# A two-block model in one kernel: parameters of a norm and splits ahead of a loop, a pair's one-hot product earlier, later posts, and products of ones in five waits

## The chip, the cores and the metric

The kernel runs on one core of one Trainium2 chip. The metric is the time of one execution on the device in microseconds, the median of several runs. Instructions run on TensorE (PE; the loads of its weights are told apart as PEld), VectorE (DVE), ScalarE (ACT) and GpSimd (POOL); SyncE (SP) issues most of the DMA transfers.

## What is computed

256 tokens of width 1024, float32, pass through two blocks of two layers each. A layer of the first block is a mixer (pooling, short convolution, attention) and a gated feed-forward, both behind an RMS norm that is modulated by a vector `c`. A layer of the second block is a mixer with three kinds of attention and then a mixture of 16 experts of width 512, each followed by a layer norm:

```python
def hybrid_layer(x, c_act, ...):                     # the first block runs it twice
    sh1, sc1, g1, sh2, sc2, g2 = jnp.split(c_act @ w_ada + b_ada, 6)
    h = rmsnorm(x, norm1_w) * (1 + sc1) + sh1
    u = h @ w_in
    ...
    x = x + g1 * (merged @ w_out)
    h2 = rmsnorm(x, norm2_w) * (1 + sc2) + sh2
    return x + g2 * ((silu(h2 @ w_gate) * (h2 @ w_up)) @ w_down)

def second_block(x, ...):
    h = layer_norm(x, ln_in_g, ln_in_b)
    for l in range(2):
        mix = mixer_sublayer(h, ...)
        h = layer_norm(ALPHA * h + mix, ln1_g[l], ln1_b[l])
        h = layer_norm(ALPHA * h + grouped_moe(h, ...), ln2_g[l], ln2_b[l])
    return h

def grouped_moe(h, ...):
    scores = sigmoid(h @ router_w)       # a group of 4 experts is chosen, then 2 of the 4
    ...
    for e in range(16):
        a = silu(h @ w_gate[e]) * (h @ w_up[e])
        y = y + dense_gates[:, e:e + 1] * (a @ w_down[e])
    return y
```

## The kernel before

The state (`st[0]`, 256 tokens as two tiles of 128 partitions) stays in SBUF. The order of PE's instructions is the order in which the program is written; a scheduler sets the order of DVE, ACT, POOL and SP. Each engine works its own instructions strictly in order. To put work of one stage into the waits of another, the program keeps a list `steps` of generators and a list `posts`; `pump` (L110) first runs all posts, then some steps.

**First block.** Products in float32 are made of two halves of higher and lower bits: weights are split by a CAST on ACT and a subtraction on DVE (L278, L279, tile `split`) and multiplied at L289, L290 and L321 to L323. `ada_pe` makes the modulation; its transposes at L685 wait for a product by DVE at L682. In the first layer (L908 on) the products of `w_in` begin behind the first modulation.

**Mixer of the second block** (`mixer`, L1193). It begins with the layer norm: `norm_params` (L806) makes scale and shift of each token out of the aggregates of statistics that were taken on the fly, `normalise` (L819) applies them on ACT and DVE, PE transposes the result (L855), and `ev` (L1202) writes it in two halves to `hl`. Then come the low-rank products of `w_in`, by L321 to L323.

**Mixture of experts** (`moe`, L1475). The routing is small work on DVE (L1506 to L1530) that ends in the masks `mb` and `mask`. Five products on PE (L1534 to L1538) count the places of the tokens in each expert, `one_hot` (L1546) makes matrices of 128 tokens by 64 places for each of four experts, and `gather` (L1562) picks the tokens with them, out of the normalised state in two halves `hn`; the lower halves are subtractions on POOL (L1502) and DVE (L1569).

The 16 experts go in 8 pairs (`pair`, L1619): the two experts' 64 places each fill the 128 partitions. `proj` (L1592) makes the gate and the up product out of 8 k-chunks of weights, the activation (L1632 to L1634) is transposed by PE (L1638) and copied by ACT (L1640), and two projections of 512 columns follow (four of 256 for the last pair), which ACT and DVE evict as two halves `yh` and `yl`, scaled by `gs` (L1671, L1672). `combine_T` (L1602) multiplies the one-hot by the gates (`go`, L1607), transposes it on PE (L1612) and derives `got` and `gs` from it. `combine` adds the pair's result to the state: a product of `got` and `yh`, `yl` (L1655) and an add on DVE (L1657). Its two steps are run by `pump` in the next pair, between L1634 and the transposes and after L1640; in the last pair, each quarter's is called from `proj` of the next quarter, behind its first k-chunk, with the statistics for the next norm (L802) behind it. The weights, 6.3 MB a pair, come in pieces of 1 MB on SP's queue (L1683) into a ring of 18 units.

If an expert has more than 64 tokens, the pairs are run again in a loop of rounds (`tc.For_i`, L1716), whose count is read from memory (L1710); in the runs here its body isn't entered, but every engine passes through its branch. `norm_params` for the next norm stands behind this loop, and at the very end the last norm with its gains (L1743 to L1761).

## Time and profile before

| | |
|---|---|
| time, median of 3 runs | 1619.72 us (1618.51 to 1620.62) |
| time of the profiled execution | 1618.68 us |
| span of its trace, first to last instruction | 1616.4 us |
| PE busy | 1510.0 us (93%), 9211 instructions |
| DVE busy | 976.5 us (60%) |
| ACT busy | 736.3 us (46%) |
| POOL busy | 251.8 us (16%) |
| DMA | 419.71 MB, 260 GB/s on average |
| mean granted clock of PE | 0.980 |

Shares are of the span. The second block begins near 841 us; its two expert stages lie from about 985 to 1219 and from about 1370 to 1602. A row of a timeline has the start of a group of like instructions, the time from the first's start to the last's end, engine, line, operation, and in brackets the idle time of the engine before it and what ended that. The granted clock is PE's: 1.00 is 2.4 GHz, 0.50 is 1.2 GHz.

### The profile page before, as it was taken

Reading aid. Unit: us, or ns where it says so; the run is one execution under the profiler, and the core shown is the slowest. Engines: PE = TensorE matmul, PEld = TensorE weight load, DVE = VectorE, ACT = ScalarE, POOL = GpSimd, SP = SyncE. Lnnn points to the kernel's source line nnn. Section 1 sums busy time; section 2 is a strip of 40 time slices with the busy share of each in tenths; the row PEclk is TensorE's granted clock in tenths of the full one; section 3 lists DMA queues with packets and bytes.
Section 4 is the critical chain, followed back from the end, with each engine's and each line's share of the span. In section 5 each row is a group of like instructions: output and inputs, shape, how many; then the busy total and the mean of one; then the engine's idle time right before and its main releaser. Section 6 shows DMA issues by size and latency. Waiting matters only on the chain. (4 is left out here: it accounts for less than half of the span.)

```text
span 1616.4 us, 24413 instructions
## 1 busy us (share of the span) xinstructions
PE 1510.0 (93%) x9211; PEld 1092.7 (68%) x9211; DVE 976.5 (60%) x1894; ACT 736.3 (46%) x1403; POOL 251.8 (16%) x279
## 2 busy tenths in 40 slices
PE   6999999999999999999989998999988998999996
PEld 5877888888887888888878775334437776344332
DVE  4869777777786767777557774322137767222224
ACT  3466645655456664556446664112115565111112
POOL 0334640001242363000003100000001210000000
PEclk9999999999999999999999998999998999999998
DMA  9766769557854675965526368999985558899992
GB/s 346 245 215 236 261 219 353 181 179 235 313 186 136 218 271 185 318 207 174 164 73 209 128 222 300 403 407 407 407 314 168 179 180 315 314 407 406 407 405 92
DMA packets 278476, 419.71 MB, mean 260 GB/s; under 512 B 12722, under 2 KB 147748, under 8 KB 278348
## 3 DMA queue, kind: packets, MB, share of 16 engines
q1 hardware_dynamic: 273052, 398.63, 69.5%
q0 software_dynamic: 5152, 19.14, 3.4%
q8 instruction: 77, 1.26, 0.3%
q14 instruction: 51, 0.42, 0.1%
q10 hardware_dynamic: 144, 0.26, 0.0%
HBM read 416.94 MB, written 1.05 MB: 259 GB/s over the span
## 5 line engine op out<-in xcount | busy, mean ns | idle before, releaser
L279 DVE TENSOR_TENSOR split<-raw,split 128x1024 fp32r<-128x1024 f32 (+4 forms) x330 | 411.7, 1251 | 114.3 <-ACT split L278 111.2
L289 PE MATMUL mm<-hl,split 128*128 128x512 f32 x1168 | 412.6, 397 | 0.0
L278 ACT CAST split<-raw 128x1024 fp32r<-128x1024 f32 (+4 forms) x330 | 328.7, 1000 | 131.6 <-PE mm L323 69.5
L290 PE MATMUL mm<-hl,split 128*128 128x256 f32 x1168 | 326.3, 279 | 1.0 <-DVE split L279 1.0
L289 PEld LDWEIGHTS mm<-hl,split 128*128 128x128 f32 x1168 | 219.0, 187 | 50.4 <-issue 0.7
L1597 PE MATMUL mm<-raw,xg 128*64 128x512 f32 x1024 | 230.9, 602 | 1.1 <-ACT xg L1564 1.1
L290 PEld LDWEIGHTS mm<-hl,split 128*128 128x128 f32 x1168 | 220.3, 189 | 1.5 <-DVE split L279 1.3
L1597 PEld LDWEIGHTS mm<-raw,xg 128*64 128x64 f32 x1024 | 71.5, 138 | 136.5 <-issue 118.7
L289 PE MATMUL mm<-ahl,split 128*128 128x512 f32 x352 | 123.4, 395 | 0.0
L306 ACT COPY t<-mm 128x256 f32<-128x256 f32 x152 | 56.4, 371 | 142.7 <-PE mm L290 133.7
L1597 PE MATMUL mm<-raw,t 128*64 128x512 f32 (+1 forms) x576 | 114.8, 549 | 1.4 <-ACT t L1640 1.4
L321 PE MATMUL mm<-split,hl 128*128 128x512 f32 (+4 forms) x272 | 102.3, 376 | 4.2 <-ACT split L278 3.2
L290 PE MATMUL mm<-ahl,split 128*128 128x256 f32 x352 | 98.3, 279 | 0.3 <-DVE split L279 0.3
L322 PE MATMUL mm<-split,hl 128*128 128x512 f32 (+4 forms) x272 | 96.4, 355 | 1.0 <-DVE split L279 1.0
L323 PE MATMUL mm<-split,hl 128*128 128x512 f32 (+4 forms) x272 | 96.4, 355 | 0.3 <-POOL hl L1210 0.2
L306 DVE TENSOR_TENSOR t<-mm,t 128x256 f32<-128x256 f32 x140 | 59.1, 422 | 47.9 <-ACT t L306 47.7
L1633 DVE SCALAR_TENSOR_TENSOR t<-t,mm 128x512 f32<-128x512 f32 x16 | 11.0, 686 | 123.3 <-ACT t L1632 123.3
L1597 PEld LDWEIGHTS mm<-raw,t 128*64 128x64 f32 x576 | 39.4, 137 | 63.8 <-issue 53.4
L1672 DVE SCALAR_TENSOR_TENSOR t<-mm,s,t 128x512 fp32r<-128x512 f32 (+1 forms) x36 | 24.9, 692 | 94.9 <-ACT t L1671 94.9
L1671 ACT ACTIVATE t<-mm,s 128x512 fp32r<-128x512 f32 (+1 forms) x36 | 23.0, 640 | 129.9 <-PE mm L1597 129.9
L289 PEld LDWEIGHTS mm<-ahl,split 128*128 128x128 f32 x352 | 66.0, 187 | 15.5 <-ACT t L1095 0.2
L1640 ACT COPY t<-at 128x512 f32<-128x512 f32 x16 | 9.4, 586 | 129.7 <-PE at L1638 129.7
(426 smaller groups left out, 2563.3 us busy)
## 6 DMA issues: line engine op xcount, KB each, us to landing
raw<-in_exp_w_gate_dram SPq DMA_DIRECT2D x128, 512.0 KB
raw<-in_exp_w_up_dram SPq DMA_DIRECT2D x128, 512.0 KB
raw<-in_exp_w_down_dram SPq DMA_DIRECT2D x128, 512.0 KB
raw<-in_w_in_dram SPq DMA_DIRECT2D x54, 1024.0 KB
raw<-in_w_ada_dram SPq DMA_DIRECT2D x30, 1024.0 KB
raw<-in_w_gate_dram SPq DMA_DIRECT2D x22, 1024.0 KB
raw<-in_w_up_dram SPq DMA_DIRECT2D x22, 1024.0 KB
ada<-in_w_ada_dram POOLq DMA_DIRECT2D x18, 1024.0 KB, 5.8
```

What stands on the lines that cost most here:

```text
L278: S.copy(h, src)
L279: V.tensor_sub(lo, src, h)
L289: PE.matmul(ps, h[:, k], x[k0 + k], start=first and k == 0, stop=False)
L290: PE.matmul(ps[:, :T], lo[:, k], x[k0 + k][:, :T], start=False, stop=last and k == K - 1)
L306: return S.copy(b[:, :T], ps[:, T:]), V.tensor_add(dst, ps[:, :T], b[:, :T])
L321: PE.matmul(ps[i][:, :n], xh, h[:, j], start=f, stop=False)
L322: PE.matmul(ps[i][:, :n], xh, lo[:, j], start=False, stop=False)
L323: PE.matmul(ps[i][:, :n], xl, h[:, j], start=False, stop=z)
L1597: PE.matmul(ps[64 * b:64 * b + 64, :], lhs(k, b), ws[k][b], start=k == 0, stop=k == nk - 1)
L1633: V.scalar_tensor_tensor(th, th, 1.0, pg, op0=OP.add, op1=OP.mult)
L1671: S.activation(yh[:, sl], pd_[:, :w], AF.Copy, scale=gs)
L1672: V.scalar_tensor_tensor(yl[:, sl], pd_[:, :w], gs, yh[:, sl], op0=OP.mult, op1=OP.subtract)
```

## The change

It has six parts. (1) `pump` runs a post only if it was there at the pump before. (2) `busy(n)` puts n products of a matrix of ones, 128x128 by 128x512 in bfloat16, on PE, into a bank that nobody reads: 12 in the first layer behind the first modulation, 12 behind the first `normalise`, 10 and 2 around the routing's products, 8 ahead of the loop of rounds, 4 behind the other `normalise`. (3) In `mixer`, the transposes of quarters 2 and 3 become steps that run between the chunks of the first low-rank product. (4) POOL's subtractions of the routing become two on DVE, one ahead of the mask's products, one behind `one_hot`. (5) `combine_T` is a generator: `go` is made at the pair's beginning, the transposes come at the fourth k-chunk of the gate product, in the last pair too; the combine of a quarter also moves to the fourth k-chunk, and the last pair pumps as the others do. (6) `norm_params` and the first splits of the next `w_in` stand ahead of the loop of rounds (and `norm_params` again in its body); in the last layer the gain banks are copied to SBUF there, and the last norm reads these copies instead of PSUM.

```diff
     def pump(n=1):
-        while posts:
+        for _ in range(min(aged[0], len(posts))):
             posts.pop(0)()
+        aged[0] = len(posts)
...
+    def busy(n, w=512):
+        pb = at_bank()
+        for _ in range(n):
+            PE.matmul(pb[:, :w], onesb, onesb[:, None, :].to_broadcast([P, w // P, P]), start=True, stop=True)
...
             ada_pe(0, 2, ada_first[2])
-            pump()
+            while posts:
+                posts.pop(0)()
+            busy(12)
...
-        transposed(ev)
+        transposed(ev, (0, 1))
+        def rest():
+            for q in (2, 3):
+                transposed(ev, (q,))
+                yield
+        steps.append(rest())
...
-        rq = rank_in(xs_gemm(k_chunks(W, l, KD, 0, 384), hl, 384), 384, cqT, 3, "mla_q")
+        rq = rank_in(xs_gemm(k_chunks(W, l, KD, 0, 384), hl, 384, 1), 384, cqT, 3, "mla_q")
...
-                    if q == 0:
-                        G.tensor_sub(hn[1][:, i, sl], y[:, i, sl], hn[0][:, i, sl])
...
+        V.tensor_sub(hn[1][:, 0, 0:512], y[:, 0, 0:512], hn[0][:, 0, 0:512])
         gained = gains(f"ln1_{l}", [mm_bank(), mm_bank()])
         next(gained)
+        busy(10)
         pp = at_bank()
...
+        busy(2)
...
         oh = one_hot(0, pos)
+        V.tensor_sub(hn[1][:, 1, 0:512], y[:, 1, 0:512], hn[0][:, 1, 0:512])
...
-                if mid and k == 1:
+                if mid and k == 3:
                     mid()
...
+            yield
             pb = at_bank()
             for i in range(2):
                 PE.transpose(pb[:, i * P:(i + 1) * P], go[:, i * P:(i + 1) * P], ident)
...
-            return got, gs[:, 0:1]
+            yield got, gs[:, 0:1]
...
-            if done:
-                got, gs = combine_T(p, oh)
+            turned = combine_T(p, oh)
+            next(turned)
+            box = []
             pg, pu = mm_bank(), mm_bank()
-            proj(pg, xs, wg, KD, more=more)
-            if done:
-                pump(2)
+            proj(pg, xs, wg, KD, lambda: box.extend(next(turned)), more)
+            got, gs = box
...
-            if not done:
-                got, gs = combine_T(p, oh)
...
+        keep = sml.tile([P, 8], F32, tag="keep", name=nm("keep"), bufs=1)
+        norm_params(keep)
+        busy(8)
+        splits[:] = U_SPLIT
+        nsplit[0] = 0
         if l + 1 < L:
-            mixer_first(l + 1)
+            wf = mixer_first(l + 1)
+            split_early(wf[0][1][:, 0:2])
+            split_early(wf[0][1][:, 2:4])
+            taken = ring["units"] + U_SPLIT[:2]
+        else:
+            lnb = unit(U_LAST, "lnb").rearrange("p (v q n) -> p v q n", v=2, q=2)
+            for q in range(2):
+                for v in range(2):
+                    pb = gain_bank(f"ln2_{l}", v, q)
+                    (S.copy if v else V.tensor_copy)(lnb[:, v, q], pb)
+            taken = (U_LAST,)
...
     normalise(*norm_params(), st.pop())
+    busy(12)
     for l in range(L):
-        moe(l, mixer(l))
+        keep = moe(l, mixer(l))
         if l + 1 < L:
-            held[:] = 3 * [normalise(*norm_params())]
-    g_, b_ = [[gain_bank(f"ln2_{L - 1}", v, q) for q in range(2)] for v in range(2)]
-    rs, nb = norm_params()
...
+            normalise(keep[:, 4:6], keep[:, 6:8])
+            busy(4)
...
-            V.scalar_tensor_tensor(t, t, mean[:, i:i + 1], g_[q], op0=OP.add, op1=OP.mult)
-            V.scalar_tensor_tensor(t, t, rs[:, i:i + 1], b_[q], op0=OP.mult, op1=OP.add)
+            V.scalar_tensor_tensor(t, t, mean[:, i:i + 1], lnb[:, 0, q], op0=OP.subtract, op1=OP.mult)
+            V.scalar_tensor_tensor(t, t, rs[:, i:i + 1], lnb[:, 1, q], op0=OP.mult, op1=OP.add)
```

The changed file has other line numbers: L1597 of before is L1616 there, L1607 is L1626, L1615 and L1616 are L1635 and L1636, L1634 is L1654, L1655 and L1657 are L1673 and L1675, L1672 is L1690, L279 is L288, L802 is L811, the aggregates of L810 are L817.

DVE within one pair of experts, before (`t_10456` is the pair's activation, `t_10483` its `go`, the adds at L1657 belong to the pair before):

```order
L1634 SCALAR_TENSOR_TENSOR t_10456<-t_10455,mm_10422 128x512
L1657 TENSOR_TENSOR state_8374<-state_8374,at_10460 128x512
L1657 TENSOR_TENSOR state_8374<-state_8374,at_10464 128x512
L1657 TENSOR_TENSOR state_8374<-state_8374,at_10475 128x512
L1657 TENSOR_TENSOR state_8374<-state_8374,at_10479 128x512
L1607 TENSOR_TENSOR t_10483<-oh_10186,gate_10204 128x128 x2
```

DVE from the activation of one pair to that of the next, after the change (`t_10623` is the next pair's `go`):

```order
L1654 SCALAR_TENSOR_TENSOR t_10506<-t_10505,mm_10465 128x512
L1675 TENSOR_TENSOR state_8387<-state_8387,at_10510 128x512
L1675 TENSOR_TENSOR state_8387<-state_8387,at_10514 128x512
L1675 TENSOR_TENSOR state_8387<-state_8387,at_10525 128x512
L1675 TENSOR_TENSOR state_8387<-state_8387,at_10529 128x512
L1690 SCALAR_TENSOR_TENSOR t_10543<-mm_10533,s_10476,t_10542 128x512
L1690 SCALAR_TENSOR_TENSOR t_10556<-mm_10546,s_10476,t_10555 128x512
L1626 TENSOR_TENSOR t_10623<-oh_10559,gate_10244 128x128 x2
L1635 TENSOR_SCALAR got_10649<-at_10646 128x256
L1636 TENSOR_REDUCE s_10650<-at_10646 128x1
```

The instruction that makes `go` has moved from behind the four adds to behind the evictions of the pair before.

PE in the last pair's projections by quarters, before (`mm_11455` is the first quarter, `mm_11468` the second, `t_11464` and `t_11465` are `yh` and `yl` of the first):

```order
L1597 MATMUL mm_11455<-raw_11369,t_11451 64x256 x8
L1597 MATMUL mm_11468<-raw_11372,t_11451 64x256 x2
L1655 MATMUL at_11471<-t_11464,got_11387 128x256
L1655 MATMUL at_11471<-t_11465,got_11387 128x256
L1655 MATMUL at_11477<-t_11464,got_11387 128x256
L1655 MATMUL at_11477<-t_11465,got_11387 128x256
L1597 MATMUL mm_11468<-raw_11372,t_11451 64x256 x6
```

And after the change:

```order
L1616 MATMUL mm_11495<-raw_11409,t_11483 64x256 x8
L1616 MATMUL mm_11508<-raw_11412,t_11483 64x256 x6
L1673 MATMUL at_11515<-t_11504,got_11435 128x256
L1673 MATMUL at_11515<-t_11505,got_11435 128x256
L1673 MATMUL at_11521<-t_11504,got_11435 128x256
L1673 MATMUL at_11521<-t_11505,got_11435 128x256
L1616 MATMUL mm_11508<-raw_11412,t_11483 64x256 x2
```

Six instead of two products of the next quarter now stand ahead of the combine (each of these rows' products at L1597 appears as two instructions in the trace).

DVE at the end of the first expert stage, before (L1710 is the read of the count of rounds, L1716 the loop's branch):

```order
L1657 TENSOR_TENSOR state_8374<-state_8374,at_11539 128x256
L802 BN_STATS s_11475<-state_8374 128x6 x2
L1710 TENSOR_LOAD nri_10215
L1716 COMPARE_AND_BRANCH
```

And after the change:

```order
L811 BN_STATS s_11519<-state_8387 128x6 x2
L817 BN_AGGR keep_11598<-s_11519 128x2
L288 TENSOR_TENSOR split_11623<-raw_11619,split_11623 128x768
L817 BN_AGGR keep_11598<-s_11519 128x2
L288 TENSOR_TENSOR split_11626<-raw_11619,split_11626 128x768
L821 TENSOR_SCALAR s_11602<-keep_11598 128x2
L823 SCALAR_TENSOR_TENSOR s_11603<-s_11601,s_11602 128x1 x2
L824 SCALAR_TENSOR_TENSOR keep_11598<-s_11603,s_11601 128x2
L825 SCALAR_TENSOR_TENSOR keep_11598<-keep_11598 128x2
L1728 TENSOR_LOAD nri_10255
L1750 COMPARE_AND_BRANCH
```

The norm's chain and two splits have moved ahead of the loop's branch, between the two aggregates and behind them.

## Rows read from the trace of the kernel before

**Rows 1.** The page, busy time of each engine over the span.

```profile
PE 1510.0 (93%) x9211; PEld 1092.7 (68%) x9211; DVE 976.5 (60%) x1894; ACT 736.3 (46%) x1403; POOL 251.8 (16%) x279
```

**Rows 2.** The waits of PE: line, releaser, us in total, times, longest.

```profile
PE at L1612 <- DVE t L1607: 18.0, 14, 1.8
...
PE at L1534 <- DVE mb L1530: 9.0, 2, 4.5
PE at L685 <- DVE t L682: 6.4, 3, 3.4
```

**Rows 3.** Timeline, a middle pair of experts, and the beginning of pair 7.

```profile
1065.64 2.65 DVE L1657 TENSOR_TENSOR state<-state,at 128x512 f32<-128x512 f32 x4
...
1068.64 0.44 PE L1612 MATMUL at<-con,t 128*128 128x128 f32 x2 [1.20 <-DVE t L1607]
...
1187.15 0.53 PE L1612 MATMUL at<-con,t 128*128 128x128 f32 x2 [1.77 <-DVE t L1607]
```

**Rows 4.** Timeline, the last pair of the first expert stage, PE.

```profile
1194.62 2.13 PE L1655 MATMUL at<-t,got 128*128 128x512 f32 x8
...
1196.69 7.09 PE L1597 MATMUL mm<-raw,xg 128*64 128x512 f32 x32
...
1204.57 0.66 PE L1638 MATMUL at<-con,t 128*128 128x128 f32 x4 [0.79 <-DVE t L1634]
...
1205.90 2.38 PE L1597 MATMUL mm<-raw,t 128*64 128x256 f32 x20 [0.68 <-ACT t L1640]
...
1214.73 1.14 PE L1655 MATMUL at<-t,got 128*128 128x256 f32 x4
...
1217.89 1.14 PE L1655 MATMUL at<-t,got 128*128 128x256 f32 x4 [0.57 <-ACT t L1671]
```

**Rows 5.** By windows: length, busy times, PE's clock, DMA share, GB/s.

```profile
1160.00:1180.00 20.00, 18.80 (x93) 8.11 (x93) 5.07 (x10) 3.27 (x6) 0.00 (x0) 1.00 1.05 407
1180.00:1200.00 20.00, 18.23 (x84) 6.70 (x82) 5.74 (x11) 1.97 (x3) 0.00 (x0) 1.00 1.07 394
1200.00:1220.00 20.00, 16.01 (x102) 8.07 (x98) 8.03 (x21) 4.06 (x7) 0.00 (x0) 1.00 0.20 73
```

**Rows 6.** Timeline, the routing of the first expert layer.

```profile
985.71 2.50 POOL L1502 TENSOR_TENSOR hn<-state,hn 128x512 fp32r<-128x512 f32 x2 [46.25 <-ACT hn L1500]
...
986.07 0.93 DVE L1524 TENSOR_TENSOR s<-s,s 128x8 f32<-128x8 f32 x1
987.03 1.22 DVE L1530 SCALAR_TENSOR_TENSOR mb<-s,s 128x32 bf16<-128x32 f32 x1
...
988.17 0.18 DVE L1530 SCALAR_TENSOR_TENSOR mask<-s,s 128x32 f32<-128x32 f32 x1
...
991.54 3.68 PE L1597 MATMUL mm<-raw,xg 128*64 128x512 f32 x8
```

**Rows 7.** The first layer's first product (timeline), and windows behind it.

```profile
27.22 0.79 PE L321 MATMUL mm<-split,hl 128*128 128x512 f32 x1 [3.25 <-ACT split L278]
...
30.00:32.00 2.00, 2.00 (x6) 1.57 (x5) 1.09 (x1) 0.00 (x0) 0.00 (x0) 0.50 1.05 410
32.00:34.00 2.00, 2.00 (x8) 1.60 (x7) 0.00 (x0) 0.70 (x1) 0.00 (x0) 0.81 1.05 409
```

**Rows 8.** Timeline, PE at the beginning of the second block's first mixer.

```profile
842.51 3.67 PE L855 MATMUL at<-con,state 128*128 128x128 f32 x16 [3.15 <-ACT state L826]
```

**Rows 9.** Timeline, behind the loop of rounds of the first expert layer.

```profile
1222.47 0.39 DVE L810 BATCH_NORM_AGGREGATE s<-s 128x2 f32<-128x24 f32 x2 [2.22 <-issue]
...
1224.86 3.68 PE L855 MATMUL at<-con,state 128*128 128x128 f32 x16 [5.83 <-ACT state L826]
...
1228.19 0.96 DVE L279 TENSOR_TENSOR split<-raw,split 128x768 fp32r<-128x768 f32 x1 [0.57 <-ACT split L278]
```

**Rows 10.** Timeline, the last norm.

```profile
1608.40 1.41 DVE L1758 SCALAR_TENSOR_TENSOR state<-state,s,at 128x512 f32<-128x512 f32 x2 [2.15 <-ACT t L1748]
...
1610.01 1.27 POOL L1750 TENSOR_TENSOR state<-state,t 128x512 f32<-128x512 f32 x1 [239.32 <-ACT state L1749]
```

More of the change, by code (lines that the diff above doesn't have):

```diff
@@ L108 @@
     steps, posts = [], []
+    aged = [0]
     def pump(n=1):
-        while posts:
+        for _ in range(min(aged[0], len(posts))):
             posts.pop(0)()
+        aged[0] = len(posts)
         while n and steps:
@@ L174 @@
     RING_MOE = (22, 8, 10, 11, 0, 12, 13, 9, 17, 18, 19, 20, 21, 5, 6, 7, 3, 4)
+    U_LAST = 12
     UNIT = {8: 2560}
@@ L802, in stats, with norm_params @@
             V.bn_stats(bs[0][:, i, 6 * q:6 * q + 6], src[i] if src else st[0][:, i, w * q:w * q + w])
-    last_mv = [None]
-    def norm_params():
-        mv = last_mv[0] = small(4).rearrange("p (a b) -> p a b", a=2)
+    def norm_params(keep=None):
+        mv = (keep[:, 0:4] if keep is not None else small(4)).rearrange("p (a b) -> p a b", a=2)
         for i in range(2):
             V.bn_aggr(mv[:, i], bs[0][:, i])
-        y, h, z, rs, nb = small(2), small(2), small(2), small(2), small(2)
+        y, h, z = small(2), small(2), small(2)
+        rs, nb = (small(2), small(2)) if keep is None else (keep[:, 4:6], keep[:, 6:8])
         S.activation(y, mv[:, :, 1], AF.Abs_reciprocal_sqrt, bias=epst[:, 2:3])
@@ L1710, in moe @@
         rounds = nc.values_load(nri[0:1, 0:1], min_val=1, max_val=4)
-        if l + 1 < L:
-            mixer_first(l + 1)
-        loop_ring = tuple(u for u in RING_MOE if l + 1 == L or u not in ring["units"])
+        keep = sml.tile([P, 8], F32, tag="keep", name=nm("keep"), bufs=1)
[3 more added lines that the diff above has]
+        nsplit[0] = 0
+        if l + 1 < L:
+            wf = mixer_first(l + 1)
[9 more added lines that the diff above has]
+            taken = (U_LAST,)
+        loop_ring = tuple(u for u in RING_MOE if u not in taken)
         first_ring = ring["units"]
@@ L1727, in moe @@
                 stats(q, new=False, n=4)
+            norm_params(keep)
         if l + 1 < L:
@@ L1730, in moe @@
             mixer_ahead(l + 1)
+            return keep
+        return keep, lnb
     first = mixer_first(0)
@@ L1735 @@
     normalise(*norm_params(), st.pop())
+    busy(12)
     for l in range(L):
-        moe(l, mixer(l))
+        keep = moe(l, mixer(l))
         if l + 1 < L:
-            held[:] = 3 * [normalise(*norm_params())]
-    g_, b_ = [[gain_bank(f"ln2_{L - 1}", v, q) for q in range(2)] for v in range(2)]
-    rs, nb = norm_params()
-    mean = small(2)
-    V.tensor_scalar_mul(mean, last_mv[0][:, :, 0], -1.0)
+            normalise(keep[:, 4:6], keep[:, 6:8])
+            busy(4)
+    keep, lnb = keep
+    mean, rs, nb = keep[:, 0:4:2], keep[:, 4:6], keep[:, 6:8]
     t = st[0][:, 1, 0:512]
-    gb = [t512() for _ in range(2)]
-    for s_, d_ in zip((g_, b_), gb):
-        S.copy(d_, s_[0])
     S.activation(t, t, AF.Identity, bias=nb[:, 1:2], scale=rs[:, 1:2])
-    G.tensor_mul(t, t, gb[0])
-    G.tensor_add(t, t, gb[1])
+    G.tensor_mul(t, t, lnb[:, 0, 0])
+    G.tensor_add(t, t, lnb[:, 1, 0])
     for q in range(2):
```

## The prediction

> **What bounds the kernel now.** I read the page's first lines, then the list of what TensorE (PE) waited for, then the timeline and the tables by stretch at each place the diff touches. PE is busy 1510.0 us of a 1616.4 us span [rows 1], so I look for the places where PE stands still or runs slowly, and ask what each edit does there. The list of waits shows three of them [rows 2]: the combine's transposes at L1612 (14 waits, 18.0 us in all), the routing's products at L1534 (two waits, 9.0) and the modulation at L685 (three, 6.4). Four more come from timelines: the first layer's first product, the beginning of each mixer, the loop's gate, and the end.
>
> The sum is made against the profiled execution, 1618.68 us; the median of the runs, 1619.72, is 1.04 above it.
>
> **Combine, 14 pairs.** Before, PE needs the transposes of `go` right after the activation's transposes and two combine steps of the pair before. VectorE (DVE) makes `go` behind four adds that hold it 2.65 us from 1065.64, and PE waits 1.20 for it; ahead of pair 7 it waits 1.77 [rows 3]. Six pairs at 1.2 and one at 1.77 make 9.0 a layer, the 18.0 of the list. After the change `go` stands on DVE right behind the previous pair's last `yl`, and PE asks for it at the fourth k of the gate projection. Eight k's take 7.09 us [rows 4], so three take 2.66. Pair 7 shows how soon `go` can be had: 1.77 us behind the product before it. So it is there before PE asks: **-18.0** (-12, if 0.4 stayed at each of the 14, to -18.0). Next late are the weights, below.
>
> **The last pair.** PE waits 0.79 at its activation transposes and 0.68 at its first down product. After the change two combine steps of pair 6 (8 products, 2.13 us, which before ran ahead of the up product) stand around these two places and fill them: 1.47 a layer, **-2.9** (0 to -2.9). The quarters of the last down product follow each other at 3.16 us (1214.73 to 1217.89). Of it 16 instructions of projection take 1.90 (20 took 2.38), and four combine products 1.14, waiting included, since they stand two products behind the quarter that they read, too early for `yl`. With six products between, that wait is covered. A combine product alone takes between 0.13 (half of one with 512 columns, 2.13 / 8) and 0.285 (1.14 / 4); at 0.2, between the two, a round is 2.7: 0.45 less, three times, and a little at the last: -1.5 a layer, **-3.0** (-0.4 to -4.4) [rows 4].
>
> **Weights.** In the experts' stage the queues move 407 GB/s, 394 between 1180 and 1200, and after 1200 only 73 x 20 us = 1.46 MB, about what the next layer's first two loads hold. So the last expert bytes land near 1200 [rows 5]. A piece of 1.05 MB takes 2.57 us at 407. Counted back over the four pieces of the last down weights, the last up piece lands near 1190; PE uses it at about 1202, at 6 of 8 k's behind 1196.69 [rows 4]. Of this slack of 11.6 us the change takes 9.0 (the waits) and 2.13 (the combine steps, now behind the up product). Half a microsecond is left; for pieces that come a little late I charge **+0.6** (0 to +11, rival B).
>
> **Routing, twice.** POOL's two subtractions hold 985.71 to 988.21. Beside them a DVE instruction of 128x8 took 0.93, and the one that makes `mb` 1.22, while its twin, the next on DVE, made `mask` in 0.18 [rows 6]. The subtractions move to DVE, one ahead of `mb` at 0.66, as one of the four adds took [rows 3]. So DVE saves 0.75 and 1.04, pays 0.66, and with some overlap lost `mb` comes 0.4 earlier, at least in the likeliest case. Then the clock: the first 8 products of the gate projection took 3.68 us [rows 6], where 8 of 32 take 1.77 [rows 4]; 12 products of ones now run in the wait of 4.5. No row shows such a product; nearest is the combine's of 128x512, 0.27, so 12 take 3.2 and fit. If they hold the clock, 1.9 comes back here and about 0.5 in the gather ahead of it: -2.8 with the 0.4. Half of the clock's part counted, -1.8 each: **-3.6** (+0.4 to -5.6).
>
> The Trainium skill, "SBUF — State Buffer", section "Who interferes with whom", has it that a VectorE instruction with two SBUF inputs and a GpSimd instruction that reads SBUF shut each other out for a whole instruction. The 0.93 and 1.22 beside 0.18 agree.
>
> **First layer and first mixer.** The first product of the first layer comes at 27.22 behind a wait of 3.25; the granted clock is 0.50 after it and 0.81 on average from 32 to 34, so it is back at about 32.8 [rows 7]. From 28 to 32.8 half speed costs 2.4. Twelve products of ones run in the wait; but the weights land at 410 GB/s all the while and can hold PE next: **-1.5** (0 to -2.5). At mixer 0, behind a wait of 3.15, 16 transposes take 3.67 [rows 8], 0.23 each, against 0.165 for the four of the last pair [rows 4]. At that pace they cost 1.0 less, at double speed 1.8; half of them also move behind the first products: **-2.0** (-0.5 to -2.7). The 12 products, 3.2, just fit the wait.
>
> **The loop's gate.** At the branch DVE stands 2.22 us, then the aggregates come at 1222.47, and PE's transposes, behind a wait of 5.83, at 1224.86; the first split on DVE at 1228.19 [rows 9]. After, the chain from the aggregates to the normalising (about 1.5 of these 2.39) and two split subtractions (2 x 0.96) stand ahead of the branch on DVE; behind it there are two split subtractions less and half the transposes ahead of the first product. So the normalising begins some 1.7 later than it would with the branch alone, less the chain and the table load that no longer follow: what is paid and what is gained nearly cancel. **-0.5** for mixer 1 (+1.5 to -2.0).
>
> **End.** The first two of six last DVE instructions take 1.41 from 1608.40, with one operand in PSUM; POOL multiplies from 1610.01 for 1.27, and adds after it [rows 10]. After, the parameters are there before the branch, and the gain banks are copied to SBUF there: some 0.85 earlier. But now both operands lie in SBUF, as in the slow pair [rows 6], and DVE can stand for up to 2 x 1.27 = 2.5. I take **+1.0** (-0.9 to +1.7). By the same section of the Trainium skill's "SBUF — State Buffer" the whole 2.5 would be paid and the sum be 0.7 higher; no run here shows it for these shapes.
>
> **Posts.** The modulation's posts come one pump later; three waits of 6.4 in all [rows 2] leave PE, but DVE and POOL set that loop's period: **-0.5** (+0.5 to -3.0).
>
> Sum: -18.0 - 2.9 - 3.0 + 0.6 - 3.6 - 1.5 - 2.0 - 0.5 + 1.0 - 0.5 = -30.4. 1618.68 - 30.4 + 1.04 = **1589.3 us**.
>
> **Rivals.**
> B, the weights bind. From about 1000 to 1190 the queue works 190 us without a break. At the 394 of its last stretch instead of 407 [rows 5] the last up piece lands 6 us later; less the 0.5 of slack, 5.5 a layer, 11 in all: 1600. For it: the slack is nearly used up. Against: 407 is steady before.
> C, the products of ones don't hold the clock. Then the 1.5 of the first layer, the 2.0 of mixer 0 and 2.8 of the routing's 3.6 fall away: 1595.6. For it: no row shows the clock under such products.
> D, slower. PE frees the ring's units at other moments than the loads want them, and the expert queue falls behind. Its point: per layer the loads come 17 us later over the 190, a rate near 374; each of the two stages then ends 5.4 later than before and, less the 7.6 that lie outside the weights' reach (1.5, 2.0, 3.6, 0.5), the kernel is 3.2 slower: 1623. At 366 it is 1631. Against: no wait that goes away holds a load back, and no window of the stage shows such a rate.
> E, all small places give their upper ends: 1.4 (quarters) + 2.0 (routing) + 1.0 + 0.7 + 1.5 + 1.9 + 2.5 = 11.0 more: 1578.
> N, it doesn't do what it says: DVE reaches `go` behind the adds again, and the 18.0 stay: 1607.3. Against: in the order `go` stands ahead of them.
>
> **Numbers.** Forecast 0.60, B 0.15, C 0.13, E 0.05, N 0.02, D 0.05 (0.03 of it beyond 0.2%). A measurement of this kernel can tell 0.2%, 3.2 us, from no change. Faster: 0.60 + 0.15 + 0.13 + 0.05 + 0.02 = 0.95; within it 0.02; slower 0.03. The range takes in C and most of B above, and reaches to E below: 1579 to 1603. Outside lie D, N, about half of E and a third of B, 0.15 in all.
>
> **What would show it.** Right: no wait at the `go` transposes, and none for a weight transfer in its place; rounds of 2.7 us in the last pair; the first gate step at 1.8 to 2 us, `mb` near 0.2, mixer 0's transposes at half their time, full granted clock near 30 us. B and D would show as waits of PE for expert weights, C as granted clock 0.5 at the same places, E as waits gone at L685. Last DVE instructions longer than 0.75 beside POOL would show the contention at the end. Waits that move from `go` to the combine's adds or the activation, so that the two stages don't shrink by some 12 us each, would make the prediction wrong.

## The result, and the profile after

The changed kernel takes 1598.73 us, the median of four runs from 1593.02 to 1602.77, beside 1619.12 for the kernel before on the same chip: a ratio of 0.9875, 95% interval 0.984 to 0.9911. It is faster, by 20 us where 30 were forecast; the time lies inside the range of 1579 to 1603 and 9.4 above the forecast. The profiled execution took 1599.32 us, its span is 1597.3. Line numbers of the changed kernel are higher than before's by 9 in the first block and by some 18 in the expert stage.

What PE waits for now (line, releaser, us in total, times, longest):

```profile
PE mm L1077 <- DVE t L1082: 6.0, 6, 1.0
...
PE at L135 <- issue: 5.5, 1, 5.5
PE mm L1079 <- DVE split L288: 4.3, 5, 1.4
...
PE mm L332 <- POOL hl L1220: 2.7, 5, 0.9
...
PE at L1551 <- DVE mb L1545: 1.5, 1, 1.5
```

The waits for `go` and, but for 0.2 us, for the modulation's product [rows 2] are gone, and of the routing's 9.0 us 1.5 are left (L1551). In their place stand six at the merged products (L1077; before, two of 1.8 in all) and 4.3 us for splits beside them (L1079), five at a mixer's first products (L332), and 5.5 us ahead of products of ones (L135) behind the loop of rounds.

The timeline of a middle pair, of the beginning of pair 7 and of the last pair:

```profile
1050.72 0.44 PE L1632 MATMUL at<-con,t 128*128 128x128 f32 x2
...
1179.48 0.48 DVE L1626 TENSOR_TENSOR t<-oh,gate 128x128 f32<-128x128 f32 x2
1180.55 0.44 PE L1632 MATMUL at<-con,t 128*128 128x128 f32 x2
...
1193.31 0.60 PE L1658 MATMUL at<-con,t 128*128 128x128 f32 x4
1193.66 1.18 PE L1673 MATMUL at<-t,got 128*128 128x512 f32 x4
1194.77 3.24 PE L1616 MATMUL mm<-raw,t 128*64 128x256 f32 x28
1197.94 0.74 PE L1673 MATMUL at<-t,got 128*128 128x256 f32 x4
...
1200.49 0.74 PE L1673 MATMUL at<-t,got 128*128 128x256 f32 x4
```

No bracket stands behind the transposes at L1632 now, where before's had 1.20 and 1.77 [rows 3]. The quarters of the last pair follow each other at 2.55 us (1197.94 to 1200.49) instead of 3.16 [rows 4], and four combine products take 0.74, as they no longer wait inside.

The routing of the first expert layer:

```profile
984.92 2.33 PE L135 MATMUL at<-onesb 128*128 128x512 bf16 x10
...
988.46 0.18 DVE L1545 SCALAR_TENSOR_TENSOR mb<-s,s 128x32 bf16<-128x32 f32 x1
...
991.92 2.59 PE L1616 MATMUL mm<-raw,xg 128*64 128x512 f32 x8
```

The products of ones fill 2.33 us of PE's wait, `mb` takes 0.18 instead of 1.22, and the first eight gate products take 2.59 instead of 3.68 [rows 6].

PE at the loop of rounds behind the first expert stage:

```profile
1204.94 1.14 PE L1673 MATMUL at<-t,got 128*128 128x256 f32 x4 [0.58 <-ACT t L1689]
1205.97 1.89 PE L135 MATMUL at<-onesb 128*128 128x512 bf16 x8
1213.36 1.89 PE L135 MATMUL at<-onesb 128*128 128x512 bf16 x4 [5.51 <-issue]
1215.05 0.85 PE L863 MATMUL at<-con,state 128*128 128x128 f32 x3
```

The next mixer's transposes begin 10.11 us behind the last combine (1204.94 to 1215.05), where before it was 6.97 (1217.89 [rows 4] to 1224.86 [rows 9]).

The windows of the end of the first expert stage (length, busy times, PE's clock, DMA share, GB/s):

```profile
1160.00:1180.00 20.00, 20.00 (x94) 7.49 (x92) 5.81 (x10) 2.56 (x4) 0.00 (x0) 1.00 1.05 407
1180.00:1200.00 20.00, 20.00 (x116) 9.20 (x114) 6.67 (x14) 3.71 (x6) 0.00 (x0) 1.00 1.07 394
```

PE is busy without a gap, where it was 18.80 and 18.23 of 20 [rows 5], and the transfers keep the same two rates. No wait of PE for expert weights is in its list.

To see where the time went I took, from the traces, the starts of the same PE instructions in two kernels, and from their differences how much each stretch got longer (+) or shorter (-) against the kernel before, in us. The stretches: **merged**, the merged products of the second layer (586 to 617); **mixer**, from the last transposes of the first block to the end of the second block's first low-rank product; **routing** 0 and 1, from the router's last product to the fourth step of the gate product; **experts** 0 and 1, from there to the last combine; **loop**, from there to the end of the next first low-rank product; **end**, from the last combine to the end of the span. "E" rows are the experiments below.

| | merged | mixer | routing 0 | experts 0 | loop | routing 1 | experts 1 | end |
|---|---|---|---|---|---|---|---|---|
| changed kernel | +3.4 | -0.3 | -1.4 | -12.7 | +6.4 | -2.5 | -11.9 | +0.3 |
| E1 no ones | +2.6 | +2.0 | -1.4 | -12.7 | +3.5 | -0.7 | -12.2 | -0.4 |
| E2 loop as before | +2.6 | -0.2 | -2.6 | -11.7 | +3.2 | -2.5 | -11.1 | +0.3 |
| E3 posts as before | -0.2 | -0.2 | -2.5 | -12.6 | +3.5 | -1.7 | -12.7 | +0.3 |
| E4 combine alone | +0.2 | -0.3 | -0.5 | -12.6 | -0.1 | +0.1 | -11.3 | 0.0 |
| E5 mixer as before | +1.1 | -1.5 | -2.6 | -12.7 | +3.0 | -2.5 | -12.3 | +0.3 |
| E6 POOL's subtractions | +2.1 | -0.2 | -1.9 | -12.7 | +3.4 | -1.1 | -12.1 | +0.8 |
| E7 end from PSUM | +2.1 | -0.3 | -2.6 | -12.7 | +3.5 | -2.5 | -12.7 | +0.8 |
| E8 four undone | -0.3 | -1.5 | -2.6 | -12.6 | +0.9 | -1.4 | -11.5 | +1.9 |
| E9 more undone | -0.3 | -1.6 | -2.6 | -12.6 | +0.1 | -2.5 | -11.3 | -0.6 |
| E10 E9, ones 8 and 4 | -0.2 | -1.5 | -2.5 | -12.6 | +3.4 | -2.5 | -12.4 | -0.6 |
| E11 E9, ones 8 ahead | -0.4 | -1.6 | -2.6 | -12.6 | +4.2 | -1.4 | -11.4 | -0.6 |
| E12 E9, ones 4 behind | +0.3 | -1.6 | -2.6 | -12.4 | +1.1 | -2.5 | -12.7 | -0.6 |

The two expert stages carry the whole gain, 24.6 us. The loop takes back 6.4 and the merged products 3.4. Between the stretches kernels also drift by up to 3.4 us where no edit lies (E11 lost 3.4 between 617 and 839 us; in E9 5.4 us in all lie outside the table), which is why the medians below scatter more than the table. The column "loop" also holds the clock's course: behind that loop PE's clock is at half for 10.2 us in the kernel before, in E8 and in E11, for 13.7 in the changed kernel, E1 and E2, and for 6.8 in the others. Half clock there doesn't always cost time: E4, with before's code there, has 3.4 us less of it and stands at -0.1.

### The profile page after: what moved, and what is told of

Read it like the earlier page. It is cut to its first block, busy times and chain, and to the rows that moved or that the text cites. A ratio compares the mean times of both kernels' runs of the same rounds, so it can differ in the third digit from the quotient of the medians.

```text
span 1597.3 us, 24586 instructions
## 1 busy us (share of the span) xinstructions
PE 1521.1 (95%) x9279; PEld 1093.1 (68%) x9279; DVE 979.0 (61%) x1899; ACT 733.6 (46%) x1401; POOL 246.2 (15%) x275
## 3 DMA queue, kind: packets, MB, share of 16 engines
q8 instruction: 77, 1.26, 0.3%
## 5 line engine op out<-in xcount | busy, mean ns | idle before, releaser
L288 DVE TENSOR_TENSOR split<-raw,split 128x1024 fp32r<-128x1024 f32 (+4 forms) x330 | 412.3, 1252 | 119.7 <-ACT split L287 116.4
L1616 PE MATMUL mm<-raw,xg 128*64 128x512 f32 x1024 | 231.9, 598 | 1.3 <-ACT xg L1582 1.3
L1616 PEld LDWEIGHTS mm<-raw,xg 128*64 128x64 f32 x1024 | 70.5, 137 | 131.1 <-issue 111.7
L1616 PE MATMUL mm<-raw,t 128*64 128x512 f32 (+1 forms) x576 | 114.8, 549 | 0.0
L332 PE MATMUL mm<-split,hl 128*128 128x512 f32 (+4 forms) x272 | 96.5, 355 | 3.3 <-POOL hl L1220 2.7
L1616 PEld LDWEIGHTS mm<-raw,t 128*64 128x64 f32 x576 | 39.4, 137 | 66.3 <-issue 51.4
L1690 DVE SCALAR_TENSOR_TENSOR t<-mm,s,t 128x512 fp32r<-128x512 f32 (+1 forms) x36 | 24.9, 692 | 87.0 <-ACT t L1689 87.0
L298 PEld LDWEIGHTS mm<-ahl,split 128*128 128x128 f32 x352 | 66.0, 188 | 15.6 <-ACT t L1105 0.2
L299 PEld LDWEIGHTS mm<-ahl,split 128*128 128x128 f32 x352 | 66.4, 189 | 0.6 <-DVE split L288 0.6
```

The source lines that it names most:

```text
L288: V.tensor_sub(lo, src, h)
L298: PE.matmul(ps, h[:, k], x[k0 + k], start=first and k == 0, stop=False)
L299: PE.matmul(ps[:, :T], lo[:, k], x[k0 + k][:, :T], start=False, stop=last and k == K - 1)
L332: PE.matmul(ps[i][:, :n], xl, h[:, j], start=False, stop=z)
L1616: PE.matmul(ps[64 * b:64 * b + 64, :], lhs(k, b), ws[k][b], start=k == 0, stop=k == nk - 1)
L1690: V.scalar_tensor_tensor(yl[:, sl], pd_[:, :w], gs, yh[:, sl], op0=OP.mult, op1=OP.subtract)
```

## The experiments

**E4, the combine alone**, on the kernel before:

```diff
-                if mid and k == 1:
+                if mid and k == 3:
...
-            if done:
-                got, gs = combine_T(p, oh)
+            turned = combine_T(p, oh)
+            next(turned)
+            box = []
...
-            proj(pg, xs, wg, KD, more=more)
-            if done:
-                pump(2)
+            proj(pg, xs, wg, KD, lambda: box.extend(next(turned)), more)
+            got, gs = box
...
```

> The kernel before with the fifth part of the change alone: the one-hot product at the pair's beginning, transposes and quarters' combine at the fourth k-chunk, no early pump in the last pair. My theory: the two expert stages give 12.1 to 12.7 us each whatever the other parts do, so about 1594.5 us (1593 to 1597). The rival, that the expert weights bind and part of the saving in the changed kernel comes from elsewhere: 1600 us or more, with waits of PE for expert weights.

Measured: 1597.27 us (1594.27 to 1602.12), ratio 0.988 (0.9852 to 0.9908). The expert stages give 12.6 and 11.3, the second less than expected, and the time is 0.3 above the expected range. One part of the change alone has the time of the whole; the other five together give nothing. The rival falls: PE waits for expert weights once, for 0.2 us, in the second stage. The same wait stands in E2, E8, E9 and E11, and these five are the kernels whose second stage gives only 11.1 to 11.5: the slack of the weights is used up there.

**E1, no products of ones**, `busy` returns at once.

> The changed kernel without any product of ones, all six places empty. My theory: the ones bring little, since what they win is taken by the next wait. In the first layer the 2.8 us won near 30 us are given back at 445 us, where PE waits for the modulation's weights; in the first mixer the eviction chain of ACT, DVE and POOL bounds the first product; in the routing the granted clock still falls, only later; at the loop's gate the four ones run at half clock and delay the transposes by 1.7. So the time stays within 2 us of the changed kernel, 1597 to 1601 us. The rival, that the ones carry a good part of the gain by holding the clock (the forecast's 6.3 us): 1604 us or more.

Measured: 1603.24 us (1601.41 to 1609.73), ratio 0.992 (0.9891 to 0.9949): between the two expectations, and by the table both are partly wrong. Without ones the mixer is 2.3 worse and routing 1 1.8, but the loop 2.9 better. In the first layer the ones do keep the clock. There the windows of the changed kernel are

```profile
30.00:32.00 2.00, 2.00 (x11) 1.64 (x10) 0.68 (x2) 1.05 (x1) 0.00 (x0) 1.00 1.05 409
32.00:34.00 2.00, 2.00 (x38) 1.45 (x36) 0.81 (x1) 0.78 (x1) 0.00 (x0) 1.00 1.05 407
```

at full clock instead of 0.50 and 0.81 [rows 7], and PE is 2.8 us ahead at 33 us. Most of it lasts: near 430 us PE is 1.9 ahead (the products with `ones` at L751 begin at 428.04; before at 429.97, without ones at 429.93), and behind a stop of 1.48 the first product of the second layer begins at 445.38, before at 446.64:

```profile
444.74 0.63 PE L704 MATMUL at<-raw,cs 128*32 128x128 f32 x12 [1.48 <-issue]
...
445.38 0.48 PE L330 MATMUL mm<-split,hl 128*128 128x512 f32 x1
```

So the theory that the gain is given back at 445 us doesn't hold. But the gain isn't safe: of the eleven kernels with ones in the first layer, E2, E5, E6, E7 and E9 have lost it by 190 us, and in these alone PE's clock is at half once more near 80 or 134 us, for 3.4 us.

**E2, the loop as before** for the first expert layer:

```diff
-        norm_params(keep)
-        busy(8)
+        if l + 1 == L:
+            norm_params(keep)
+        busy(0 if l + 1 < L else 8)
...
-            wf = mixer_first(l + 1)
-            split_early(wf[0][1][:, 0:2])
-            split_early(wf[0][1][:, 2:4])
+            mixer_first(l + 1)
...
-            normalise(keep[:, 4:6], keep[:, 6:8])
-            busy(4)
+            held[:] = 3 * [normalise(*norm_params())]
```

> The changed kernel with the first expert layer's norm parameters and the two splits behind the loop of rounds again, as before, and no products of ones there; the last layer keeps them ahead. My theory: the chain and splits ahead of the branch hold it for all engines, and this costs 6.9 us between the last statistics and the end of the next first low-rank product; undone, the time falls by 6 to 7.5 us, to about 1592. The rival, that those 6.9 us come from what follows the gate in any case (transposes as steps, weights): less than 2.5 us.

Measured: 1596.01 us (1593.21 to 1601.79), ratio 0.9864 (0.9832 to 0.9896); the loop's stretch is 3.2 shorter, between the theory's 6 to 7.5 and the rival's 2.5. My theory that the chain and the splits hold the branch at that price falls: E1, with chain and splits but no ones, is only 0.3 above E2. What is left, 3.2, lies behind the branch, which PE passes as before:

```profile
1213.38 1.97 PE L863 MATMUL at<-con,state 128*128 128x128 f32 x8 [5.83 <-ACT state L834]
1216.72 0.69 PE L330 MATMUL mm<-split,hl 128*128 128x384 f32 x1 [1.37 <-ACT split L287]
```

The first low-rank product comes 10.3 us behind the last combine in both kernels, but here PE has waited 1.37 for a split where before it made the other half of the transposes, which now follow. And PE stands at half clock for as long as in the changed kernel; no run parts these two. The windows of the changed kernel are

```profile
1211.70:1225.40 13.70, 11.12 (x34) 8.39 (x35) 6.16 (x12) 5.41 (x10) 1.46 (x2) 0.50 0.73 252
```

while E3, with the changed kernel's code at this place, has half clock for 6.8 us only, and +3.5 instead of +6.4 (E6 and E7 likewise):

```profile
1209.20:1216.00 6.80, 5.10 (x16) 2.99 (x16) 2.59 (x6) 3.34 (x6) 0.00 (x0) 0.50 0.95 317
1216.00:1222.90 6.90, 6.18 (x38) 5.70 (x37) 5.02 (x10) 3.34 (x7) 2.03 (x3) 1.00 0.50 189
```

So 3 of the 6.4 belong to the clock's course in the one execution that was profiled, and some 3.5 to the code.

**E3, posts as before**: `while posts: posts.pop(0)()`.

> The changed kernel with posts run at the next pump, as before. My theory: the wait at the modulation's transposes only moved to the merged products, whose period DVE and POOL set, and the later posts cost 2.3 us in the second layer: 1595.5 to 1598, that is 1 to 3 us less than the changed kernel. The rival, that later posts won what the forecast counted for them: 0.5 to 3 us more than the changed kernel.

Measured: 1594.88 us (1592.88 to 1596.98), ratio 0.986 (0.9841 to 0.9879). The time is a little below the expected range. The merged products are 3.6 shorter than in the changed kernel; in all six kernels with later posts this stretch is 1.1 to 3.4 longer than before, in the seven without them -0.4 to +0.3. The wait at the modulation had only moved: with posts as before PE waits 6.7 us there again, and with later posts six waits at L1077, each ended by DVE (L1082), and those for splits take its place. That the later posts put the modulation's DVE work at a worse place in that loop, whose period DVE and POOL set, is how I read it; no run shows it by itself.

**E5, the mixer as before**: `transposed(ev)` for all quarters, no steps between the first product's chunks.

> The changed kernel with all four quarters of a mixer's transposes ahead of the first low-rank product again, and no steps run between its chunks. My theory now: what follows the gate was lost to the transposes as steps, since the products then wait for the halves that ACT, DVE and POOL make one quarter at a time. So the stretch from the last transposes of the first block to the end of the first low-rank product gets some 2 us shorter, and the stretch of the first product to that end behind the gate 2 to 4 us: 4 to 6 us in all, to about 1593.5. The rival, that the half clock behind the gate alone costs this: under 1.5 us.

Measured: 1594.34 us (1592.68 to 1594.91), ratio 0.9832 (0.9813 to 0.9851). The mixer is 1.2 shorter; the loop at equal clock (6.8 us at half, beside E3) only 0.5. So the theory misses, with 1.7 instead of 4 to 6; that the time is near its 1593.5 comes from the clock at the loop (3.0) and from stretches that this edit doesn't touch. With steps PE waits for POOL's half of `hl` (L1220) instead of for its own transposes.

**E6, the routing's subtractions on POOL again.**

> The changed kernel with the routing's two subtractions on POOL again, the products of ones kept. My theory: the mask is held by the pair of DVE and POOL as before, some 0.8 us in each layer, and the longer wait lets the clock fall earlier: 1 to 3 us more than the changed kernel in both layers together. The rival, that the ones alone made the routing's gain: no change beyond 0.5 us in the two stretches of the routing.

Measured: 1599.28 us (1598.48 to 1602.72), ratio 0.9868 (0.9847 to 0.989). The routings lose 0.7 and 1.4 against the usual -2.6 and -2.5, as expected; against the changed kernel's own execution it is 0.9 in all. Of the usual gain of 5.1 some two fifths are POOL's, since 2.1 go without its part (here) and 2.1 stay without the ones (E1).

**E7, the last norm from PSUM**: DVE's gain banks made by PE behind the loop.

> The changed kernel with the last norm's DVE instructions reading the gain banks from PSUM again, made by PE behind the loop; only POOL's two operands are copied to SBUF ahead of it. My theory: beside POOL the DVE instruction with both operands in SBUF stands for POOL's whole instruction; undone, the first two of them take 1.4 instead of 3.4 us and the stretch from the last combine to the end gets 1.3 to 2 us shorter. The rival, that DVE begins later then, since PE leaves the branch late: no shorter, within 0.5 us.

Measured: 1597.17 us (1595.29 to 1603.98), ratio 0.9858 (0.9825 to 0.989); the end is 0.5 longer, so the rival holds. Yet the contention is there. The timeline of the changed kernel's end, and then of this one's:

```profile
1588.06 1.26 POOL L1784 TENSOR_TENSOR state<-state,lnb 128x512 f32<-128x512 f32 x1 [272.37 <-ACT state L1783]
1588.12 3.42 DVE L1792 SCALAR_TENSOR_TENSOR state<-state,keep,lnb 128x512 f32<-128x512 f32 x2 [2.04 <-ACT state L1783]
1589.40 1.59 POOL L1785 TENSOR_TENSOR state<-state,lnb 128x512 f32<-128x512 f32 x1
```

```profile
1588.96 2.07 PE L841 MATMUL at<-lnrow,lnsel 64*128 64x512 f32 x4 [5.37 <-POOL state L1785]
...
1589.79 1.41 DVE L1793 SCALAR_TENSOR_TENSOR state<-state,keep,at 128x512 f32<-128x512 f32 x2 [5.14 <-PE at L841]
```

Two instructions with both operands in SBUF take 3.42 beside POOL, and 1.41 from PSUM: 2.0 lost. But PE comes out of the branch 5.37 us after its last instruction, so DVE begins 2.5 later behind the last combine (which starts at 1580.88 in the changed kernel and 1580.05 here). The Trainium skill's exclusive lock ("SBUF — State Buffer", "Who interferes with whom") agrees with the 3.42.

**E8, four things undone**: posts, mixer, no ones at the loops, end from PSUM.

> The changed kernel with four things undone together: posts at the next pump, transposes of a mixer all ahead, no products of ones at the two loops, the last norm from PSUM. My theory: the single prices add up, 3 + 2 + 3 + 2.5 + 1.5 us: 1584 to 1590. The rival, that one bound (the weights' transfers, the clock) takes most of it back: 1593 or more.

Measured: 1590.04 us (1587.48 to 1593.0), ratio 0.9805 (0.9781 to 0.9828). That is the upper end of the expected range. The single prices nearly add up, but the end cost 1.9 here: PE came out of the last branch 8.2 us after its last instruction. The chain and two splits ahead of the branch, without ones, stand at +0.9 in the loop: they gain nothing.

**E9, the loop as before too, and the last norm on DVE alone**, so without POOL and without PSUM:

```diff
-    S.activation(t, t, AF.Identity, bias=nb[:, 1:2], scale=rs[:, 1:2])
-    G.tensor_mul(t, t, lnb[:, 0, 0])
-    G.tensor_add(t, t, lnb[:, 1, 0])
...
-            if (q, i) == (0, 1):
-                continue
...
```

> Posts at the next pump, a mixer's transposes all ahead, the first expert layer's norm parameters and splits behind its loop as before, no products of ones at the loops, and the whole last norm on DVE from SBUF without POOL; the rest as in the changed kernel. My theory: behind the first loop it behaves as the kernel before (within 0.5 us from the last combine to the end of the next first low-rank product, where the changed kernel lost 6.4), the posts give 3 us and mixer 0 1.3, and without POOL the six instructions become eight of 0.7 us, so that the end is 0.5 to 1 us shorter: 1585.5 to 1590 us. The rival, that what is undone comes back at the next wait: 1592 or more.

Measured: 1591.01 us (1586.25 to 1592.83), ratio 0.9817 (0.9798 to 0.9837), a little above the expected range. By stretches it does what was expected: loop +0.1, mixer -1.6, merged -0.3, end -0.6, 0.9 less than in the changed kernel.

**E10, E9 with 8 ones ahead of the loop and 4 behind it.**

> The kernel of the run before with 8 products of ones ahead of the first loop and 4 behind the normalising, the norm parameters still behind the loop. My theory: PE stands only some 2 us at the branch then, the clock falls later or not at all, and the transposes behind the gate come at full clock: 1 to 3 us less behind the gate than without ones. The rival, which the changed kernel speaks for: PE comes out of the branch late and at half clock, the four products delay the transposes, and it is 1 to 2.5 us slower there.

Measured: 1589.57 us (1588.73 to 1592.75), ratio 0.9824 (0.9807 to 0.9842); the loop costs 3.3 more than in E9, so the rival holds, by more than it said: the transposes begin 10.13 us behind the last combine instead of 6.97. This is the price of the ones at this place, without the chain and the steps, and the half clock is as long as in E9. The medians don't show it, as E10's is 1.4 below E9's: the drift between the stretches is larger, and this price is read from one execution of each kernel.

**E11 and E12, each of the two groups of ones alone.**

> The kernel of e9_best with 8 products of ones ahead of the first loop, and none behind it. My theory: ones ahead of the branch cost nothing, since PE has to wait for the norm there anyway, and only those behind it stand in the way of the transposes: from the last combine to the end of the next first low-rank product no more than 0.7 us above the kernel before. The rival, that the ones ahead hold the branch for all engines: 1.5 us or more above it.

> The kernel of e9_best with 4 products of ones behind the first loop's normalising, and none ahead of it. My theory: PE comes out of the branch late, runs the four at half clock ahead of the transposes, and these start 2.5 to 3.5 us later than in e9_best. The rival: PE is out of the branch in time, and the four fill the wait: within 0.7 us of e9_best in this stretch.

Measured: E11 1592.76 us (1592.38 to 1596.46), ratio 0.9845 (0.9829 to 0.9862), loop +4.2; E12 1588.41 us (1587.56 to 1589.08), ratio 0.9813 (0.9796 to 0.9829), loop +1.1. Both theories missed, and E12's rival too. PE at the loop in E9, E11 and E12, in this order:

```profile
1204.50 1.14 PE L1665 MATMUL at<-t,got 128*128 128x256 f32 x4 [0.57 <-ACT t L1681]
1211.47 3.46 PE L862 MATMUL at<-con,state 128*128 128x128 f32 x15 [5.83 <-ACT state L833]
```

```profile
1202.09 1.89 PE L134 MATMUL at<-onesb 128*128 128x512 bf16 x8
1209.24 1.75 PE L862 MATMUL at<-con,state 128*128 128x128 f32 x7 [5.26 <-DMA raw<-in_w_in_dram]
1213.63 2.08 PE L862 MATMUL at<-con,state 128*128 128x128 f32 x9 [2.63 <-issue]
```

```profile
1201.68 1.14 PE L1665 MATMUL at<-t,got 128*128 128x256 f32 x4 [0.57 <-ACT t L1681]
1208.19 1.89 PE L134 MATMUL at<-onesb 128*128 128x512 bf16 x4 [5.36 <-DVE s L824]
```

In E11 as in E12 the transposes begin 1.2 us later behind the last combine than in E9 (8.18 instead of 6.97). The rest of E11's +4.2 is for the most part a stop of 2.63 in the middle of its transposes, so the figure doesn't show that ones ahead cost more than ones behind, and E11's rival (1.5 or more) got its number by that stop.

Across the branch PE stands 5.26 to 5.53 us wherever no later norm holds it, whatever releaser the row names: so too in the changed kernel (5.51), E3, E5 to E7, E10 and at before's last loop (5.51). With the norm behind the loop and no ones it stands 5.83 (in E1 and E8, with the norm ahead, 6.26 and 6.27, ended by the normalising on ACT). So PE has only 0.3 to 0.6 to spare. The 8 ones ahead of the branch (1.89) push its first instruction behind it by 1.2; the 4 behind it run at half clock and take 1.7 (1213.36 to 1215.05 in the changed kernel), of which 1.2 are not covered in E12. With both groups little is covered, and the transposes come 3.2 later (E10).

What holds PE there stands in the trace. In all 28 passes of these loops (two in each of 14 kernels) one branch instruction on PE's queue lasts 3.3 to 3.9 us; the branches of the other engines take under 0.1. In each of the 28 one transfer of 16 KB on queue q8, of the kind that the page lists as "instruction", begins 0.9 to 1.5 us after this branch and ends 1.3 to 1.6 before it is over. Twelve semaphore instructions follow, 1.2 to 1.3 us from the first to the last in 27 passes. In the changed kernel the branch lies from 1208.05 to 1211.71 and the transfer from 1208.98 to 1210.31. E11's stop of 2.63, to 1213.63, has such a transfer as well, which ends at 1212.32; so has E8's 8.2, where a second one ends at 1578.99 and PE goes on at 1580.39; and so has the stop of 1.48 in the first block, to 444.74, with one that ends at 443.39. PE goes on 1.3 to 1.4 us behind the end of each.

By the Trainium skill, "Runtime: NRT & Kernel Launch", section "Instruction fetch mechanics", a taken branch to a place that has not been fetched makes the engine fetch instructions before it goes on. The trace agrees, with 28 of 28; no run put the code behind the loop at another place, so the price of the fetch alone isn't tested.

## Why the prediction was right, and where not

The time lies in the range because the range is 24 us wide. The mechanism that was to give most of the gain did so to within 1.3 us; two steps, the loop's gate and the posts, missed by 6.9 and 3.9, together more than the 9.4 between forecast and time.

- **Combine and last pair.** Forecast -18.0, -2.9, -3.0 and +0.6 for the weights, -23.3; measured -24.6, and -23.9 for E4. The waits at the transposes of `go` went as the working says, and three k's covered them; the quarters came at 2.55 where 2.7 was worked out. The slack of the last weights, half a microsecond by the count, was enough in the first stage, and rival B didn't come: 394 and 407 stand as before. In five kernels the second stage shows it used up, with a wait of 0.2 (E4). A pair's weights, for that count, are twelve pieces of 1 MB; the 6.3 MB named with the kernel are those of one expert.
- **Routing.** Forecast -3.6, measured -3.9 in the profiled execution and -5.1 in most others. Both of its reasons hold; the ones give the larger share (E6, E1).
- **The loop's gate** failed: forecast -0.5 with an upper bound of +1.5, measured +6.4. The term put the products of ones at nothing, without a reason: the 12 at mixer 0 and in the routing were weighed against their waits, the 8 and 4 at the loop against none. The step that says "the normalising begins some 1.7 later", and that gain and loss nearly cancel, was about right for chain and splits (+0.9 in E8, and E1 beside E2 0.3). The time went to the ones, 3.3 us by E10 and 2.9 by E1, as PE's way through the branch leaves next to nothing to cover them, and to another 3 of half clock in this execution.
- **Posts** failed: forecast -0.5 (+0.5 to -3.0), measured +3.4 and undone in E3 (1.0 of it comes back by 640 us, in the products behind). The step named the reason itself, "DVE and POOL set that loop's period", and still took a gain from it; a wait that another engine's period sets moves when its instruction is moved, and what moves along is work of the engine that sets it.
- **First mixer** was mis-sized: -2.0 forecast, -0.3 measured. The clock part is right: 8 transposes take 1.09 us there now, 0.14 each instead of 0.23 [rows 8], and with all of them ahead it gives -1.5 (E5). The half that moves behind the first products cost 1.2 instead of giving something.
- **First layer.** The clock came back as forecast (2.8 us at 33 us), and the -1.5 came: near 430 us PE is 1.9 ahead (without ones 0.0 in E1 and 0.6 in E4). What takes it in five other kernels is not the bound that the term named, transfers; half clock near 80 or 134 us goes with it (E1). From 445 us on the drift is as large as this term.
- **End.** Forecast +1.0, measured +0.3. The contention costs 2.0 of the 2.5 that the term allowed; leaving out PE's way through the branch, which the step didn't count, gives most of it back.
- **Rival C** (the ones don't hold the clock) is wrong for the first layer and mixer 0, where they hold it, and for most of the routing (half clock for 3.4 us instead of 10.2 in the first). The measured time near its 1595.6 and B's 1600 is neither's doing.

## What to carry to other kernels

Work that a wait covers costs nothing only as long as the engine isn't needed right behind it: filler ahead of a branch adds to the path what it is longer than the engine's spare time there, 1.2 of 1.89 us in E11, as soon as the engine's way through takes about as long as the work that it waits for. Look for the engine that sets a loop's period before moving a wait in it; the wait of another engine isn't time to be won. When a change of many parts is timed, try the largest part alone: here it has the whole gain, and versions without later posts and without a mixer's transposes as steps (E8, E9, E10 and E12, ratios 0.9805 to 0.9824) beat both kernels.

## What was not expected of the hardware

- PE needs 5.26 us at least, in 14 kernels, from its last instruction ahead of this loop's branch to its first behind it, and 8.17 once; 3.3 to 3.9 of it are one branch instruction, with a transfer of instructions in each. DVE has 2.0 to 2.7 us at the same place, where it doesn't wait for PE, and 4.43 once (E4's last loop).
- At one and the same place, with the same code, half clock lasted 6.8 us in three executions and 13.7 in the changed kernel's, and cost 3.0 us. What decides it stays open.
- Two DVE instructions with both operands in SBUF took 3.42 us beside POOL instead of 1.41, and POOL's second 1.59 instead of 1.26.
- The lead won in the first layer is gone by 190 us in five of the eleven kernels with ones there, those where PE's clock is at half near 80 or 134 us; ahead of that PE had been idle for the most part (in E5 it was busy for 1.14 of 3.4 us).
- Why equal code drifts by up to 3.4 us between 617 and 839 us from one kernel to another stays open too; no run was made for it.
